# Batched matmul on one core: x loaded behind the weights of its group, and cast by row pairs ahead of the copies of that group

## The chip, the cores and the metric

The kernel runs on one core of one Trainium2 chip. Times are device microseconds of one launch. A run is "fast" or "slow" by its granted clock and span. Each comparison was made on one chip in alternating rounds. A ratio is the mean time of one kernel's fast runs over that of the kernel before in the same rounds, so it is not quite the ratio of the medians that are quoted.

## The reference

128 independent products of a 256 x 512 matrix by a 512 x 384 matrix, all float32:

```
b1, b2, m, k, n = 8, 16, 256, 512, 384
x: (b1, b2, m, k)   weight: (b1, b2, k, n)
out = np.matmul(x, weight).astype(np.float32)
```

x has 67.1 MB, the weights 100.7 MB, the output 50.3 MB: 218 MB that must pass between HBM and the core.

## The kernel before

Four products make a group (G = 4), so there are 32 groups. One group is one x tile (2.10 MB), two halves of weights (1.57 MB each) and one output tile (1.57 MB). All transfers are issued by SyncE, in one queue, in the order of the program; what is issued may run ahead of the computation as far as buffers allow (two x tiles, four weight halves, four output tiles).

```
def load(e, t, U, s):
    n = t * U + s
    if not isinstance(n, int) or n >= XS:
        e.wait_ge(x_cast, n + (1 - XS))
    e.dma_start(x_sb[s % XS][:], ...).then_inc(x_in[s % XS], 16)
    for d in range(G // D):                      # two halves of the weights
        ...
            e.wait_ge(w_cast, ...)
        e.dma_start(w_sb[slot][:], ...).then_inc(w_in[slot], 16)

def on_sync(e):
    ...
        for s in range(U):
            load(e, t, U, LAG + s)               # LAG = 4
            store(e, t, U, s)
```

So the queue holds x, weights, weights, store, again and again. ScalarE casts x of the next group between two output copies of the group at hand:

```
def cast_x(e, t, U, s):                          # two instructions of 2048 elements
    e.wait_ge(x_in[s % XS], ...)
    e.wait_ge(t_made, n * T + ((1 - BS) * T + BIAS))
    for h in range(S):
        ins = e.copy(out=x_bf[s % BS][:, :, h], in_=...)
    ins.then_inc(x_cast, 1)

def step(t, U, s, more):                         # ScalarE, one group
    for q in range(T):                           # T = 4 row pairs
        copy_out(e, t, U, s, q)
        if q == 1 and more:
            cast_x(e, t, U, s + 1)
```

TensorE transposes the cast x (16 instructions a group, by way of PSUM tile `pt`), VectorE copies the transposed x back (`x_t`) and casts the weights (`w_bf`), TensorE multiplies into PSUM tile `po` (128 matmuls a group), and ScalarE copies the result out (`out_sb`), from which it is stored.

## Time and profile before

| | before |
|---|---|
| time, median of 3 runs | 519.87 us (519.76 to 519.98) |
| span of the profiled run | 517.8 us |
| packets' share of 16 DMA engines' span | 99.3% |
| mean rate | 421 GB/s |
| TensorE, VectorE, ScalarE busy | 61%, 63%, 41% |

The columns are line, engine, operation, output and input, count; then the busy time in us and the mean ns of one; then the idle time ahead of them and what ended it:

```profile
L182 PE MATMUL po<-w_bf,x_t 128*32 128x384 bf16 x4096 | 231.4, 400 | 121.4 <-DVE x_t L155 121.4
...
L168 PE MATMUL pt<-identity,x_bf 128*128 128x128 f32 x512 | 82.8, 325 | 74.3 <-ACT x_bf L131 74.3
L131 ACT CAST x_bf<-x_sb 128x2048 bf16<-128x2048 f32 x64 | 118.5, 1901 | 7.3 <-DMA x_sb<-in_x_dram 7.3
...
L131 ACT ACT_TABLE_LOAD x1 | 1.3, 1283 | 1.3 <-PEq L232 1.3
```

TensorE waits for the transposed x before its matmuls (121.4 us over 32 groups), and ScalarE hardly ever waits for x (7.3 us, once, at the start), because x arrives ahead of its weights.

### The profile page before, as it was taken

What the parts mean: (1) busy time and instruction counts of PE and PEld (TensorE: products, weight loads), DVE (VectorE), ACT (ScalarE), POOL (GpSimd) and SP (SyncE); (2) the same over time, 40 slices, a digit from 0 to 9 for tenths busy, and PEclk for the clock granted to TensorE, in tenths of its full rate; (3) what the DMA queues carried; (4) which work ended last, traced back from release to release, by engine and by line L of the source; (5) the groups of instructions that cost most, each with busy time, mean ns of one, the idle gap of its engine ahead of it and who ended that gap; (6) DMA issues with size and microseconds to landing.
All of it is one profiled execution on the core that took longest, in us unless ns stands there. A gap on an engine that the chain in (4) does not pass through costs nothing.

```text
span 517.8 us, 11229 instructions
## 1 busy us (share of the span) xinstructions
PE 314.3 (61%) x4608; PEld 198.2 (38%) x4608; DVE 323.9 (63%) x384; ACT 212.9 (41%) x193; POOL 0.7 (0%) x6
## 2 busy tenths in 40 slices
PE   0588674576655676555766557665566655676653
PEld 0455443343433443333434334343344333443432
DVE  0788867655577555775556765557755577555670
ACT  3156462454324553245533345523455233553332
POOL 0000000000000000000000000000000000000000
PEclk9988896787868886787878678866877686777867
DMA  8999999999999999999999999999999999999995
GB/s 332 433 423 428 425 431 429 429 431 424 428 431 430 428 427 429 429 429 430 431 424 431 429 433 426 426 431 427 432 429 428 427 430 428 432 430 426 428 430 233
DMA packets 18869, 218.18 MB, mean 421 GB/s; under 512 B 2096, under 2 KB 2096, under 8 KB 2608
## 3 DMA queue, kind: packets, MB, share of 16 engines
q1 hardware_dynamic: 18864, 218.11, 99.3%
q8 instruction: 3, 0.05, 0.0%
q14 instruction: 2, 0.02, 0.0%
HBM read 167.77 MB, written 50.33 MB: 421 GB/s over the span
## 4 chain that ended last, share of the span: by engine, by line
DMA 81%; DVE 13%; issue 2%; PE 2%; ACT 1%; SPq 0%; DVEq 0%; ACTq 0%
DMA w_sb<-in_weight_dram 81%; DVE w_bf L149 12%; PE po L182 2%; ACT x_bf L131 0%; DVE x_t L155 0%; SPq L109 0%; ACT out_sb L196 0%; SPq L101 0%; DVEq L144 0%; DVEq L226 0%; SPq L108 0%; ACTq L195 0%; SPq L290 0%; SPq L55 0%
## 5 line engine op out<-in xcount | busy, mean ns | idle before, releaser
L149 DVE CAST w_bf<-w_sb 64x1536 bf16<-64x1536 f32 x256 | 244.5, 955 | 179.1 <-DMA w_sb<-in_weight_dram 172.1
L182 PE MATMUL po<-w_bf,x_t 128*32 128x384 bf16 x4096 | 231.4, 400 | 121.4 <-DVE x_t L155 121.4
L196 ACT COPY out_sb<-po 128x768 f32<-128x768 f32 x128 | 99.4, 803 | 289.3 <-PE po L182 289.3
L182 PEld LDWEIGHTS po<-w_bf,x_t 128*32 128x32 bf16 x4096 | 124.8, 116 | 225.3 <-DVE x_t L155 131.1
L168 PE MATMUL pt<-identity,x_bf 128*128 128x128 f32 x512 | 82.8, 325 | 74.3 <-ACT x_bf L131 74.3
L131 ACT CAST x_bf<-x_sb 128x2048 bf16<-128x2048 f32 x64 | 118.5, 1901 | 7.3 <-DMA x_sb<-in_x_dram 7.3
L168 PEld LDWEIGHTS pt<-identity,x_bf 128*128 128x128 f32 x512 | 73.3, 213 | 86.1 <-issue 86.1
L155 DVE COPY x_t<-pt 128x1024 bf16<-128x1024 bf16 x128 | 79.4, 683 | 1.0
L131 ACT ACT_TABLE_LOAD x1 | 1.3, 1283 | 1.3 <-PEq L232 1.3
masks.py:199 POOL TENSOR_SCALAR_AFFINE_SELECT identity<-identity 128x128 f32<-128x128 f32 x1 | 0.3, 294 | 0.2 <-POOL identity L202 0.2
L202 POOL MEMSET identity<- 128x128 f32 x1 | 0.2, 205 | 0.5 <-SPq L55 0.5
L279 POOL MEMSET const-bfloat16-1.0<- 128x1 bf16 x1 | 0.1, 102 | 0.0
L279 POOL MEMSET const-uint8-127<- 128x1 uint8 x1 | 0.1, 102 | 0.0
L279 POOL MEMSET const-float32-0.0<- 128x1 f32 x1 | 0.1, 99 | 0.2 <-issue 0.2
L279 POOL MEMSET const-float32-1.0<- 128x1 f32 x1 | 0.1, 99 | 0.0
## 6 DMA issues: line engine op xcount, KB each, us to landing
w_sb<-in_weight_dram SPq DMA_DIRECT2D x64, 1536.0 KB, 27.5
x_sb<-in_x_dram SPq DMA_DIRECT2D x32, 2048.0 KB, 25.8
out_dram<-out_sb SPq DMA_DIRECT2D x31, 1536.0 KB, 30.6
out_dram<-out_sb SPq DMA_DIRECT2D x4, 384.0 KB, 4.0
```

The source lines that it names most:

```text
L131: ins = e.copy(out=x_bf[s % BS][:, :, h], in_=x_sb[s % XS][:].rearrange("p r (q s c) -> p r s q c", s=S, c=KO)[:, :, h],)
L149: e.tensor_copy(out=w_bf[(s * G + d * D + a) % WBS][h * HP : (h + 1) * HP], in_=w_sb[slot][a * HP : (a + 1) * HP, h * KO : (h + 1) * KO, : ...
L155: e.tensor_copy(out=x_t[s % TS][:, 2 * q : 2 * q + 2], in_=pt[(s * T + q) % PT][:].bitcast(bf16),).then_inc(t_copied, 1)
L168: ins = e.transpose(pt[(s * T + q) % PT][:, rr, h, :], words[:, 2 * q + rr, h :: KO // 2], identity[:],)
L182: ins = e.matmul(po[(s * T + q) % PO][mine, rr, :N], x_t[s % TS][:, 2 * q + rr, ko // 2, mine, ko % 2], w_bf[(s * G + i) % WBS][:, ko, :], ...
L196: e.copy(out=out_sb[s % OS][:, 2 * q : 2 * q + 2, :], in_=po[(s * T + q) % PO][:, :, :N],).then_inc(o_copied, 1)
L202: e.memset(identity[:], 0.0).then_inc(id_done, 1)
L279: nc = _bacc.Bacc("TRN2", target_bir_lowering=False, num_devices=1)
```

## The change

The intent: a store is to be followed by weights and not by x, and x is to be cast where it is used, in four pieces of a row pair each, so that TensorE can start on the first piece. The diff, cut to its core:

```
     def load(e, t, U, s):
         n = t * U + s
-        if not isinstance(n, int) or n >= XS:
-            e.wait_ge(x_cast, n + (1 - XS))
-        e.dma_start(x_sb ...)
         for d in range(G // D):
             ...                                  # weights, unchanged
+        if not isinstance(n, int) or n >= XS:
+            e.wait_ge(x_cast, n * T + (1 - XS) * T)
+        e.dma_start(x_sb ...)

-    def cast_x(e, t, U, s):                      # whole group, two halves
+    def cast_x(e, t, U, s, q):                   # one row pair
+        if q == 0:
+            e.wait_ge(x_in[s % XS], ...)
+        e.wait_ge(t_made, n * T + (q + 1 - T + BIAS))
+        rows = slice(2 * q, 2 * q + 2)
+        e.copy(out=x_bf[s % BS][:, rows], in_=...).then_inc(x_cast, 1)

     def multiply(e, t, U, s):
-        e.wait_ge(x_cast, n + 1)
         for q in range(T):
+            e.wait_ge(x_cast, n * T + (q + 1))

     # ScalarE
-        cast_x(e, 0, NG, 0)
-        with e.Fori(0, NG // U - 1) as t: ...    # copies 0, 1, cast of the next group, copies 2, 3
+        with e.Fori(0, NG // U) as t:
+            for s in range(U):
+                for q in range(T):
+                    cast_x(e, t, U, s, q)
+                for q in range(T):
+                    copy_out(e, t, U, s, q)
```

## The prediction

> **What bounds the kernel now.** I read the page first, then the windows view by stage, then the waits of the compute engines and of the DMA queue, and last the timeline of one group in the middle. The page:
>
> ```profile
> span 517.8 us, 11229 instructions
> ...
> PE 314.3 (61%) x4608; PEld 198.2 (38%) x4608; DVE 323.9 (63%) x384; ACT 212.9 (41%) x193; POOL 0.7 (0%) x6
> ...
> DMA  8999999999999999999999999999999999999995
> ...
> DMA packets 18869, 218.18 MB, mean 421 GB/s; under 512 B 2096, under 2 KB 2096, under 8 KB 2608
> ...
> q1 hardware_dynamic: 18864, 218.11, 99.3%
> ...
> DMA 81%; DVE 13%; issue 2%; PE 2%; ACT 1%; SPq 0%; DVEq 0%; ACTq 0%
> ```
>
> The reader is to see three things. No compute engine is busy over 63%. The DMA row is 9 in 38 of 40 slices, and packets fill 99.3% of the 16 engines' span. The chain is 81% DMA. A chain can run through a transfer that only queues, so the share of DMA in it would not be enough alone; the windows view settles it:
>
> ```profile
> 4.00:30.00 26.00, 10.73 (x144) 7.15 (x144) 14.06 (x17) 7.78 (x6) 0.00 (x0) 1.00 1.01 429
> 30.00:60.00 30.00, 20.91 (x324) 15.08 (x328) 25.50 (x31) 15.72 (x15) 0.00 (x0) 0.88 1.00 425
> ...
> 100.00:490.00 390.00, 242.62 (x3508) 150.21 (x3512) 247.73 (x295) 159.22 (x145) 0.00 (x0) 0.77 1.01 429
> ...
> 505.00:517.80 12.80, 4.95 (x100) 2.60 (x92) 0.00 (x0) 3.23 (x4) 0.00 (x0) 0.77 0.56 231
> ```
>
> The last two columns are the DMA share and GB/s: 1.01 and 429 through the whole middle, so the engines never run out of packets there. One group moves 2.10 MB of x, 3.15 MB of weights and 1.57 MB of output, 6.82 MB in all; at 429 GB/s that is 15.9 us, and the timeline's period between two groups' stores is 16.1 us. In the trace's packet records a weight or store packet (12,288 bytes) takes 460 ns and an x packet (16,384 bytes) 611 ns almost without exception: all time above those minima adds up to 3.1 us per engine over the run, 1 us of it in the first 20 us. So no gap shows where a store is followed by x.
>
> The queue is also far ahead of the need:
>
> ```profile
> w_sb<-in_weight_dram SPq DMA_DIRECT2D x64, 1536.0 KB, 27.5
> x_sb<-in_x_dram SPq DMA_DIRECT2D x32, 2048.0 KB, 25.8
> out_dram<-out_sb SPq DMA_DIRECT2D x31, 1536.0 KB, 30.6
> ```
>
> A weight half moves in 3.7 us (1.57 MB at 429 GB/s), yet lands 27.5 us after its issue. Some 24 us, one and a half groups, stand in the queue before it. The issuing engine waits long (258.2 us for the x casts, 136.1 us for the weight casts in its waits), but while it waits the queue has work.
>
> **What the Trainium skill says.** "DMA: Bandwidth & Descriptors", section "Where 436 GB/s comes from", gives 435.2 GB/s as the ceiling of the ports between DMA engines and SBUF. "HBM Reference", section "Specifications (TRN2)", gives some 358 GB/s per core where both cores of a pair stream and about 425 for a core alone. The trace agrees with the second case: 429 GB/s with one core running, 1.4% under the ceiling. The DMA page's "Queues, rings and completion order" says that an engine consumes its descriptors in ring order; the landings agree, x, weights and store following one another at the pace of their bytes. "ScalarE: Activation LUTs", section "What ACT_TABLE_LOAD costs", gives 186 ns + 0.833 ns per element for an instruction with immediate operands, and some 93 ns of overlap back to back. For 2048 elements that is 1892 ns; the page of the profile has 1901 for the x cast, and two in a row take 3.70 us, so both agree.
>
> **The change, part by part.**
>
> 1. The order of loads: weights, x, store instead of x, weights, store. Bytes, packet sizes, the number of transfers and the single queue stay. Cost on the bounding resource: 0, unless a change of direction or size between packets costs something, and above it did not.
>
> 2. The x cast: two instructions of 2048 elements become four of 1024. By the skill's formula one takes 186 + 853 = 1039 ns (estimate); four in a row 4 x 1.04 - 3 x 0.09 = 3.9 us, against 3.70. That is 0.2 us per group, 6 us of ScalarE over 32 groups, on an engine 41% busy: not on the path.
>
> 3. Where the cast stands. Before, the cast of group n+1 stood after the second output copy of group n. Now the cast of n+1 follows all four copies of n. This makes a ring through ScalarE and TensorE: casts, transposes, matmuls, copies, next casts. The middle of the run gives the terms:
>
> ```profile
> 252.29 3.70 ACT L131 CAST x_bf<-x_sb 128x2048 bf16<-128x2048 f32 x2
> 253.95 7.86 DVE L149 CAST w_bf<-w_sb 64x1536 bf16<-64x1536 f32 x8 [5.50 <-DMA w_sb<-in_weight_dram]
> 255.89 1.50 ACT L196 COPY out_sb<-po 128x768 f32<-128x768 f32 x2
> ...
> 261.84 2.48 DVE L155 COPY x_t<-pt 128x1024 bf16<-128x1024 bf16 x4
> ...
> 262.58 8.02 PE L182 MATMUL po<-w_bf,x_t 128*32 128x384 bf16 x128 [4.28 <-DVE x_t L155]
> ```
>
> Ring: casts 3.9, the last row pair's transposes 0.6 (a quarter of 2.2), matmuls 8.0 (6.7 to 8.2 over the groups, as the granted clock varies), last copy 0.8, and some 0.1 for each of four hand-overs: 13.7 us. The transfers need 16.1. So the new serial ring fits, with 2.4 us to spare.
>
> 4. Does everything arrive in time? Call T the landing of a group's last load. Before, that is the second weight half: VectorE casts its four pieces until T + 4, copies the first transposed pair (0.7), and matmuls start at about T + 5. After, it is x: ScalarE casts until T + 4.0, the last transposes end at T + 4.7, and the transposed copies run beside the casts because VectorE is already through with the weights (halves land at T - 8.5 and T - 4.9, and eight casts take 7.9). Matmuls start at T + 4.8. The gain is 0.2 us and counts once, at the end of the run: the last load lands at 497.3 us, matmuls start at 502.3.
>
> 5. Buffers. Weight slots come free at about T - 4.6 and T - 0.7, x at T + 4.1, where before x came first. All are issued with well over 15 us of queue still before them (at T the queue still holds two stores and one whole group, 19.5 us, and then the new weights). At the head, I stepped through the first six groups: the least backlog I find is some 10 us. The before kernel has two slight dips near 36 and 43 us, 0.15 us together, which go.
>
> 6. The end: after the last load the stores of four older groups are queued (4 x 3.7 = 14.6 us, until about 512), so the tail too is mostly bytes; the last quarter of the last store follows the last copy.
>
> Sum: 0 in the middle, -0.15 at the head, -0.2 at the end, so 519.87 - 0.35 = **519.5 us**.
>
> **The rivals.**
>
> - *The serial ring becomes the bound.* For it: the cast and the copies now share one order with nothing between to fill TensorE, and the granted clock falls to 0.7 in places. Against it: 13.7 of 16.1 us. If I had forgotten 3.5 us per group, 1.1 us x 32 = 35 us would be lost, +7%. I think it unlikely, since every term was read from the trace.
>
> - *x frees its buffer late, the queue runs dry.* For it: the DMA queue's longest wait is already for the x cast, in-order issue makes weights and stores wait behind it, and x now needs its cast 4 us after landing. Against it: 24 us of queue. A dry queue of 0.5 us per group would make 16 us, +3%.
>
> - *The DMA engines run faster with a store followed by weights* (the intent). For it: packets of the same size follow each other there. Against it: packets already stand at their minimum; even at the ceiling of 435 GB/s the middle would gain 1.4%, 7 us. So this can hardly reach 2%.
>
> - *The transfer order is hidden altogether*: same time within 0.1%. That is close to my own sum, and likeliest.
>
> **Range and chances.** The three runs before lie within 0.22 us. Both small terms are under 0.5 us; packet service could move by some tenths of a per cent in either direction, and the tail by a us. I take 517.8 to 521.2. Faster by over 2% (below 509.5) is below what all bytes need at the present rate (218.2 MB at 429 GB/s is 508.6, plus 2 us before the first packet and 3 after the last): chance 0.01. Slower by over 2% needs one of the first two rivals: 0.03. Within 2%: 0.96.
>
> **What would show it.** DMA share 1.01 and 429 GB/s again between 100 and 490 us, packets at 460 and 611 ns (steps 1, 5). Casts x128 at about 1.04 us (step 2). ScalarE's wait for x a few us in every group, TensorE's transposes then following the casts, and matmuls some 4.8 us after x lands (steps 3, 4). VectorE waiting for transposes instead of only for weights. The prediction is wrong if the DMA row shows 7 or 8 in the middle (a dry queue or the ring), if ScalarE never waits for x (the ring is the bound), or if the packets' own times change.

## The result, and the profile after

| | before | after |
|---|---|---|
| time, median of 4 runs | 519.92 us (519.76 to 519.98) | 518.66 us (518.09 to 519.12) |
| ratio | | 0.9976 (95%: 0.9958 to 0.9993) |
| span of the profiled run | 517.8 us | 517.2 us |
| TensorE, VectorE, ScalarE busy | 61%, 63%, 41% | 59%, 64%, 46% |

A second measurement, in the rounds of the first experiments, gave 519.80 and 518.77 us, ratio 0.9980 (0.9966 to 0.9993). The change gains 0.20 to 0.24 per cent, 1.0 to 1.3 us. The predicted time was 519.5 us, a gain of 0.35.

The middle of the run in the windows view of the changed kernel (columns: window and its length, then busy us and count of TensorE's matmuls, its weight loads, VectorE, ScalarE and GpSimd, then the granted clock, the DMA share and GB/s):

```profile
100.00:490.00 390.00, 239.35 (x3556) 156.70 (x3558) 254.31 (x294) 181.25 (x203) 0.00 (x0) 0.78 1.01 429
```

The last two numbers are those of the kernel before: 1.01 and 429. The lines of the page that answer to those shown of before:

```profile
L166 PE MATMUL pt<-identity,x_bf 128*128 128x128 f32 x512 | 123.7, 425 | 199.3 <-ACT x_bf L132 199.1
L180 PE MATMUL po<-w_bf,x_t 128*32 128x384 bf16 x4096 | 185.1, 342 | 1.0 <-issue 1.0
...
L132 ACT CAST x_bf<-x_sb 128x1024 bf16<-128x1024 f32 x128 | 124.4, 1042 | 80.9 <-DMA x_sb<-in_x_dram 80.8
...
L132 ACT ACT_TABLE_LOAD x8 | 10.3, 1283 | 42.9 <-DMA x_sb<-in_x_dram 42.9
```

TensorE's wait has moved from the matmuls (121.4 us before, now 1.0) to the transposes (199.3 us), which now follow x directly. The matmuls became shorter (400 to 342 ns) and the transposes longer (325 to 425 ns). The Trainium skill explains it in "TensorE: Matmul & The Clock Gate", section "Part 1: The HAM clock gate (the "warmup" mystery)": after an idle window of some 3.4 us TensorE runs at half clock until it has been busy for about as long. The trace agrees: before, the idle 4 us stood in front of the matmuls, and in the group whose matmuls start at 278.65 us the trace's clock record is at 0.5 from 278.2 to 281.6 us, over the first 3 us of them; now the idle time stands in front of the transposes, and in the group shown next the record is at 0.5 from 272.5 to 279.3 us, over all the transposes and the first 0.9 us of the matmuls. None of this work is itself on the path that sets the time; when it runs will matter below.

One group in the middle of the changed kernel's timeline (start, length, what; in brackets the idle time ahead of it and its end):

```profile
273.31 3.89 ACT L132 CAST x_bf<-x_sb 128x1024 bf16<-128x1024 f32 x4 [2.41 <-DMA x_sb<-in_x_dram]
274.49 3.97 PE L166 MATMUL pt<-identity,x_bf 128*128 128x128 f32 x16 [4.44 <-ACT x_bf L132]
...
278.39 5.81 PE L180 MATMUL po<-w_bf,x_t 128*32 128x384 bf16 x128
```

The casts start when x lands, the first transposes follow 1.2 us later, and the matmuls begin 5.1 us after the landing.

**Where does the gain come from?** Not from the mean rate, which is the same. The end of the run shows it. Windows view of the kernel before, last columns granted clock, DMA share, GB/s:

```profile
505.00:511.00 6.00, 4.95 (x100) 2.60 (x92) 0.00 (x0) 3.23 (x4) 0.00 (x0) 0.84 0.91 377
511.00:513.00 2.00, 0.00 (x0) 0.00 (x0) 0.00 (x0) 0.00 (x0) 0.00 (x0) 1.00 0.77 306
513.00:516.00 3.00, 0.00 (x0) 0.00 (x0) 0.00 (x0) 0.00 (x0) 0.00 (x0) 0.62 0.07 30
```

and of the changed kernel:

```profile
505.00:511.00 6.00, 1.87 (x48) 1.01 (x40) 0.00 (x0) 1.72 (x3) 0.00 (x0) 1.00 0.99 410
511.00:513.00 2.00, 0.00 (x0) 0.00 (x0) 0.00 (x0) 0.00 (x0) 0.00 (x0) 0.60 0.48 191
```

A DMA share of 0.07 is one engine of sixteen (0.06) at work: in the last 3 us of the kernel before, essentially one engine still has packets and the others have none. **The time is set by the last of the 16 DMA engines, and one engine is late.** Each transfer adds 16 to its semaphore, one for each engine, and the trace records the landings. From them I take for every transfer the lag: the last of the 16 landings less their median. (The trace does not name the engine of a landing, so "the late engine" is whichever is last.) Groups and stores are counted from 0. For the last load of the last group:

```
                        median of 16 engines     last engine     lag
before (weights)              493.85 us           497.25 us      3.4 us
after  (x)                    493.76 us           496.55 us      2.8 us
last store: before 516.4 us, after 515.8 us
```

The median engine gains 0.1 us, the late engine 0.7, and that is what the profiled runs differ by (0.6). The lag of before is 1.5 us in the first group, stays there until about group 12, and then grows by 0.1 us a group; after, it stays at 1.7 to 1.8 us until about group 20. So the question for the experiments is what makes the late engine lose more time.

### The profile page after: what moved, and what is told of

It is laid out like the page before. It is cut to its first block, busy times and chain, and to the rows that moved or that the text cites. A ratio compares the mean times of both kernels' runs of the same rounds, so it can differ in the third digit from the quotient of the medians.

```text
span 517.2 us, 11523 instructions
## 1 busy us (share of the span) xinstructions
PE 306.6 (59%) x4608; PEld 200.6 (39%) x4608; DVE 332.8 (64%) x384; ACT 236.7 (46%) x264; POOL 0.7 (0%) x6
## 4 chain that ended last, share of the span: by engine, by line
DMA 81%; ACT 10%; PE 4%; issue 3%; ACTq 0%; SPq 0%
DMA x_sb<-in_x_dram 81%; ACT x_bf L132 9%; PE po L180 2%; PE pt L166 1%; ACTq L130 0%; ACT out_sb L194 0%; SPq L111 0%; SPq L103 0%; ACT L132 0%; ACTq L193 0%; SPq L282 0%; SPq L55 0%
## 5 line engine op out<-in xcount | busy, mean ns | idle before, releaser
L166 PE MATMUL pt<-identity,x_bf 128*128 128x128 f32 x512 | 123.7, 425 | 199.3 <-ACT x_bf L132 199.1
L180 PE MATMUL po<-w_bf,x_t 128*32 128x384 bf16 x4096 | 185.1, 342 | 1.0 <-issue 1.0
L166 PEld LDWEIGHTS pt<-identity,x_bf 128*128 128x128 f32 x512 | 91.8, 216 | 232.1 <-issue 218.3
L194 ACT COPY out_sb<-po 128x768 f32<-128x768 f32 x128 | 102.2, 798 | 147.2 <-PE po L180 147.2
L153 DVE COPY x_t<-pt 128x1024 bf16<-128x1024 bf16 x128 | 88.4, 691 | 122.3 <-PE pt L166 121.8
L132 ACT CAST x_bf<-x_sb 128x1024 bf16<-128x1024 f32 x128 | 124.4, 1042 | 80.9 <-DMA x_sb<-in_x_dram 80.8
L180 PEld LDWEIGHTS po<-w_bf,x_t 128*32 128x32 bf16 x4096 | 108.8, 101 | 73.8 <-issue 14.2
L132 ACT ACT_TABLE_LOAD x8 | 10.3, 1283 | 42.9 <-DMA x_sb<-in_x_dram 42.9
## 6 DMA issues: line engine op xcount, KB each, us to landing
w_sb<-in_weight_dram SPq DMA_DIRECT2D x64, 1536.0 KB, 27.5
x_sb<-in_x_dram SPq DMA_DIRECT2D x32, 2048.0 KB, 27.5
```

The lines of the kernel that those rows point to most:

```text
L132: e.copy(out=x_bf[s % BS][:, rows], in_=x_sb[s % XS][:, rows].rearrange("p r (q s c) -> p r s q c", s=S, c=KO),).then_inc(x_cast, 1)
L153: e.tensor_copy(out=x_t[s % TS][:, 2 * q : 2 * q + 2], in_=pt[(s * T + q) % PT][:].bitcast(bf16),).then_inc(t_copied, 1)
L166: ins = e.transpose(pt[(s * T + q) % PT][:, rr, h, :], words[:, 2 * q + rr, h :: KO // 2], identity[:],)
L180: ins = e.matmul(po[(s * T + q) % PO][mine, rr, :N], x_t[s % TS][:, 2 * q + rr, ko // 2, mine, ko % 2], w_bf[(s * G + i) % WBS][:, ko, :], ...
L194: e.copy(out=out_sb[s % OS][:, 2 * q : 2 * q + 2, :], in_=po[(s * T + q) % PO][:, :, :N],).then_inc(o_copied, 1)
```

## The experiments

Twelve kernels ran. Three theories stood at first: the order of packets (a store followed by weights costs the late engine less), the place of the casts, and the start (weights as the first transfers).

### One half of the change at a time

**order_only**: the kernel before with only the two blocks of `load` exchanged; the casts keep their place and their two instructions.

```
     def load(e, t, U, s):
         n = t * U + s
-        (x block)
         for d in range(G // D): ...
+        (x block)
```

> The kernel before with the new load order alone (weights, x, store); the cast stays where it was. Packet-order theory (the lagging DMA engine loses less per group where a store is followed by weights): most of the gain is here, ratio 0.9965 to 0.9985, about 518.7 us. Cast theory (the place of the casts gives the gain): ratio 0.9995 to 1.0005. Start theory (weights as the first transfers start faster): ratio about 0.998, with the gain already there when group 8's loads have landed.

Measured: 518.09 us (518.03 to 518.59, 5 runs) against 519.80, ratio 0.9971 (0.9957 to 0.9984).

**casts_only**: the changed kernel with x put back in front of the weights in `load`; the casts are by row pairs ahead of the copies.

> The changed kernel with the old load order (x, weights, store). Packet-order theory: ratio 0.9995 to 1.001, no gain. Cast theory: ratio 0.997 to 0.9985. Start theory: no gain.

Measured: 520.21 us, ratio 1.0009 (0.9995 to 1.0023).

**after_again**: the changed kernel in the same rounds.

> The changed kernel once more, on the same chip and in the same rounds as the three others. All theories: ratio 0.996 to 0.999, about 518.7 us. If it comes out within 0.9995 to 1.0005, the gain of the first measurement was chance.

Measured: 518.77 us (518.56 to 518.82), ratio 0.9980 (0.9966 to 0.9993). So the gain is no chance, it belongs to the order of the loads, and the new place of the casts adds nothing to it. The order alone is, if anything, better than the whole change: all its runs but one lie below all of the changed kernel's in the same rounds. The start theory expected the gain to be there when group 8 has landed; the median and last engines of the changed kernel stand at the same time as before there (127.9 and 129.7 against 127.9 and 129.5 us, by the last packets of that group's loads), so by this measure it falls. The measure sees only the engine that is last at that moment; what it misses is told under "The same measure in every kernel".

**store_before_x**: the changed kernel, but each store is issued between the weights and the x of a later group. The ring of transfers is then weights, weights, store, x: as a ring the same as before, though the x that follows the store now belongs to the group whose weights went ahead.

```
                 load(e, t, U, LAG + s)           # weights alone
                 store(e, t, U, s)
+                load_x(e, t, U, LAG + s)
```

> The changed kernel with the store issued between a group's weights and the next x, so that in the ring of transfers a store is followed by x again (weights, weights, store, x), as in the kernel before, though x still comes behind its own weights. Packet-order theory: no gain, ratio 0.9995 to 1.0005, and the slowest DMA engine loses some 0.03 us more per group than in the changed kernel. Cast theory and start theory: ratio about 0.998.

Measured: 530.21 us (530.01 to 530.61), ratio 1.0202 (1.0188 to 1.0216). **All three theories fell here**: one had expected no gain, two a gain, none 10 us of loss. The windows view shows the loss, and who has it:

```profile
100.00:490.00 390.00, 231.91 (x3456) 151.02 (x3456) 247.61 (x287) 177.21 (x198) 0.00 (x0) 0.77 1.01 428
504.00:508.00 4.00, 2.32 (x60) 1.23 (x48) 3.84 (x6) 2.17 (x3) 0.00 (x0) 1.00 0.14 59
...
511.50:520.00 8.50, 7.24 (x76) 4.75 (x80) 2.77 (x4) 4.68 (x5) 0.00 (x0) 0.57 0.06 25
```

In the middle all is as ever (1.01, 428 GB/s). At the end one engine works alone for 8.5 us (0.06). Its part of the last x landed only at 511.5 us, 14.2 us behind the median, and TensorE's last group had to wait for it. Its lag was 1.9 us in the first group and 14.2 us in the last. While it is alone the packet records can only be its own: its store packets of 12,288 bytes take 464 to 531 ns, where the median packet of this size takes 460.

### What slows the late engine: what follows the store, or where it stands against the computation?

**store_mid**: the kernel before, casts untouched, with the store between the two weight halves: x, weights, store, weights. A store is then followed by weights, though x comes first.

```
-                load(e, t, U, LAG + s)
-                store(e, t, U, s)
+                load(e, t, U, LAG + s, ("x", 0))
+                store(e, t, U, s)
+                load(e, t, U, LAG + s, (1,))
```

> The kernel before, casts where they were, with the store moved between the two halves of the weights: x, weights, store, weights. If what follows a store decides (x is bad, weights are good), ratio 0.996 to 0.9985 although x comes first. If it is x behind its weights that helps, ratio 0.9995 to 1.001. If the store's distance to the last load of a group decides (a store issued into the middle of a group is bad, as in store_before_x), slower, ratio 1.01 to 1.03.

Measured: 528.90 us, ratio 1.0177 (1.0163 to 1.0191); the lag grew from 1.5 to 12.4 us. So it is not what follows the store. In both orders tried, a store that stands ahead of the group's last load is bad, be that load x or weights. The computation is timed by the landing of the last load, so this says at which moment of the computation the late engine stores.

**transfers_store_x** and **transfers_store_w**: all casts, matmuls and copies taken out, stores of zeros, each load waiting only for the landing of the one before it in its buffer (results wrong). They differ in one line:

```
-        ORDER = [0, 1, 's', 'x']
+        ORDER = [0, 1, 'x', 's']
```

> The transfers alone, result wrong on purpose: no casts, no matmuls, the stores write zeros; each load waits only for the landing of the load before it in its buffer. Order weights, weights, store, x. If the late DMA engine is slowed by the other transfers alone, its lag grows here too (the last of 16 engines ends 5 us or more behind the median, run 8 to 15 us longer than its sister with store and x exchanged). If it is slowed by the compute engines' use of the buffers, the lag stays at 2 us and both orders take the same time within 0.1%. The bytes alone need 508.6 us at 429 GB/s.

> The transfers alone, result wrong on purpose, in the changed kernel's order: weights, weights, x, store. Under both theories the lag stays at about 2 to 3 us, and the run takes some 513 to 517 us; what tells them apart is the difference to the sister run.

Measured: 517.79 us (517.33 to 518.26) and 517.24 us (517.03 to 517.82), 0.1% apart, and in both the lag ends below 2 us. Without computation the two orders are worth the same; the 11.4 us that tell store_before_x from the changed kernel come with the computation. The pair also gives a floor: the changed kernel is 1.4 to 1.5 us over its transfers alone (taken on another chip, where the kernel before took 519.69 us).

### Which engine?

transfers_store_x once more, each time with one compute engine running the kernel's own kind of instruction on spare tiles, tied to no transfer (results wrong): TensorE the matmuls, VectorE the weight casts, ScalarE the output copies.

```
+    def busy(e):                                  # transfers_and_matmuls
+        with nc.Fori(0, 42, engines=...) as t:
+            for s in range(2):
+                for q in range(T):
+                    e.wait_ge(p_made, ...)        # its own earlier work
+                    (the 32 matmuls of a row pair, on tiles of zeros)
```

> transfers_store_x with TensorE alone running matmuls of the kernel's shape on tiles of zeros, tied to no transfer, through nearly the whole run; result wrong on purpose. transfers_store_x took 517.8 us with a lag of the last DMA engine of 1.9 us. If TensorE's reading of the buffers stretches the late engine's stores: lag of 5 us and more, 5 to 20 us longer. If it is another engine, or if none alone does it: 517 to 519 us, lag about 2 us.

> transfers_store_x with VectorE alone running the weight casts on a spare tile, tied to no transfer; result wrong on purpose. If VectorE's traffic stretches the late engine's stores: lag of 5 us and more, 5 to 20 us longer. If it is TensorE or ScalarE: 517 to 519 us.

> transfers_store_x with ScalarE alone running the output copies into spare tiles, tied to no transfer; result wrong on purpose. If ScalarE's traffic stretches the late engine's stores: lag of 5 us and more, 5 to 20 us longer. If it is TensorE or VectorE: 517 to 519 us.

Measured: with matmuls 528.34 us (528.10 to 528.86); with casts 517.57 us (517.33 to 517.67); with copies 517.94 us (median of 517.47, 517.84, 518.05 and one run of 521.08). **TensorE alone adds 10.5 us to the transfers, VectorE's casts and ScalarE's copies nothing that shows.** (The lags of the last two end at 2.3 and 2.7 us against 1.9, one trace each: some tenths of a us are not excluded.) Windows views of transfers_and_matmuls (columns here: TensorE's matmuls, its weight loads, GpSimd, clock, DMA share, GB/s):

```profile
50.00:460.00 410.00, 410.00 (x10100) 263.67 (x10096) 0.00 (x0) 1.00 1.01 428
...
511.00:514.00 3.00, 0.00 (x0) 0.00 (x0) 0.00 (x0) 0.50 0.23 98
514.00:525.00 11.00, 0.00 (x0) 0.00 (x0) 0.00 (x0) 0.50 0.06 26
```

and of transfers_store_x (GpSimd, clock, DMA share, GB/s):

```profile
50.00:460.00 410.00, 0.00 (x0) 1.00 1.01 428
...
511.00:514.00 3.00, 0.00 (x0) 1.00 0.44 188
514.00:516.00 2.00, 0.00 (x0) 1.00 0.03 12
```

Again one engine stands alone, for 11 us. Two details make the cause firm. The matmuls of this probe stop at 469.6 us, and the lag, which had grown by half a us a group from group 9 on, stops growing with them: 12.4, 13.0, 13.0, 13.0, 13.0 us for x of groups 27 to 31. And while the engine works alone after that, all its 23 store packets from 514 to 524.5 us take 460 ns: it is no slow engine, it is slow beside matmuls (464 to 531 ns in store_before_x). What of TensorE's work does it, reading tiles or writing PSUM, is not told apart. The fetching of its instructions is unlikely, as far as the trace records it: the instruction queues have four packets after the start.

### The same measure in every kernel

From the landings I took, for stores 8 to 27, how long the last engine needs for a store (its landing less the last landing of the transfer ahead), and from the trace how much of that time TensorE was busy. That share is taken 0.6 us earlier than the landings, since a landing is recorded some 0.5 us after the end of its packets (the last x of store_before_x: 511.00 and 511.48 us). It is rough: without the shift it is 0.25 for before and 0.57 for after.

```
kernel                   last engine's store   TensorE busy in it   its lag at store 8 / 27   median time
order_only                    3697 ns               0.00                2.2 / 2.2 us          518.09
transfers_store_x             3703 ns               0.00                1.6 / 1.9             517.79
two_more_casts                3721 ns               0.18                1.8 / 3.1             519.65
after_again                   3716 ns               0.41                1.7 / 2.6             518.77
after                         3728 ns               0.41                1.7 / 2.9             518.66
before                        3751 ns               0.41                1.7 / 3.4             519.80
casts_only                    3782 ns               0.65                2.0 / 4.3             520.21
transfers_and_matmuls         4081 ns               0.85                4.5 / 12.9            528.34
store_mid                     4076 ns               0.96                4.0 / 12.3            528.90
store_before_x                4155 ns               0.97                4.4 / 14.2            530.21
```

The more of its store lies beside TensorE's work, the longer it takes.

The last landing hides something, though: it need not be the same engine's all the time. Sort the 16 landings of each store and follow them from store to store (one trace of each kernel), and four stand apart. Before, at store 3, they are 1.25, 1.44, 1.50 and 1.53 us behind the median. At store 27 three of them are where they were (1.37, 1.44, 1.51), and the first has grown to 3.44, by 0.09 us a group; it passed the others at about store 7. After, the growing one goes from 0.72 to 2.85 us (0.50 to 2.58 in after_again), also by 0.09 us a group, and passes the others, at 1.7 to 2.0 us, at store 17 to 21. So the later onset of the lag after the change is a lower start and not a slower loss. From store 3 to 27 the growing engine loses, in ns a group: order_only 27 (it ends at 1.57 us and is never the last), two_more_casts 71, after_again 87, after 89, before 91, casts_only 128, and the three slow kernels at the foot 440 to 525 once it is last. Up to casts_only this rises with the share of TensorE in the table, and before and after agree in both. In transfers_and_matmuls the loss too starts before it shows: from 75 us on each group has a burst of 7 to 10 store packets of some 520 ns.

The three that stay behind are no matter of the stores: before, the trace has packets of 16 KB of the instruction queue at 6.2, 35.3 and 42.9 us, some 1.0 to 1.1 us each, and in the landings that follow each one more engine stands 1.5 us behind.

This gives the sizes. In order_only the growing engine ends at 1.57 us and not at 3.44, 1.5 us of it by the smaller loss ((91 - 27) ns x 24 groups). The last is then one of the three others, at 2.2, so some 1.2 us are left; the profiled spans differ by 1.5 and the medians by 1.7. For the changed kernel the loss a group is the same as before; of its gain of 1.0 to 1.3 us the lower start gives 0.5 to 0.75 (at store 3).

Why order_only is all but free of it can be read from its timeline. There the late engine's store follows its x directly and needs 3.7 us. ScalarE casts the whole x in that time, and TensorE idles:

```profile
257.92 3.70 ACT L131 CAST x_bf<-x_sb 128x2048 bf16<-128x2048 f32 x2 [4.01 <-DMA x_sb<-in_x_dram]
...
261.74 3.44 PE L168 MATMUL pt<-identity,x_bf 128*128 128x128 f32 x16 [6.09 <-ACT x_bf L131]
```

In the changed kernel the transposes begin 1.2 us after the first cast starts (the lines of group 273.31 above), so they run beside the second half of the store. By this reading (the pieces of the cast were not varied alone) the finer casts, which were to help, give back a part of what the order gains.

What stays open: that TensorE slows one engine's stores is shown, and that the order alone takes most of this loss away; but before and after lose the same, and no run says what sets the start that differs. Before, at 91 us, the growing engine falls back by 0.74 us at the moment of a packet of 8 KB of the instruction queue; two_more_casts, which loads in the order of the changed kernel, stands at 1.4 us at store 3, so the order alone doesn't set it. Whether weights as the first transfers matter is therefore not settled: when group 8's loads have landed, the growing engine of the changed kernel does stand 0.5 to 0.7 us better than before. Nor do the runs say why one engine alone is hit by TensorE, and its stores above all.

### The two rivals of the prediction

**two_more_casts** and **eight_more_casts**: the changed kernel with casts of the same size to spare tiles ahead of the real ones, in the ring of casts, transposes, matmuls and copies.

```
         rows = slice(2 * q, 2 * q + 2)
+        for v in range([1, 1, 0, 0][q]):          # eight: [2, 2, 2, 2]
+            e.copy(out=spare[...][:], in_=x_sb[s % XS][:, rows]...)
```

> The changed kernel with two casts more per group, to spare tiles, in the ring of casts, transposes, matmuls and copies: 2.0 us more in a ring that the changed kernel's trace shows to wait some 3.4 us per group for x. If the ring has that slack: same time, ratio to before 0.997 to 1.0, and the wait for x falls to about 1.5 us per group. If the serial ring were near the bound: up to 2.0 x 32 = 64 us longer, ratio up to 1.12.

Measured: 519.65 us, ratio 1.0002 (0.9986 to 1.0017), at the upper edge of what the slack was to give. ScalarE's waits for x:

```profile
ACT spare L134 <- DMA x_sb<-in_x_dram: 28.5, 16, 2.8
ACT L134 <- DMA x_sb<-in_x_dram: 27.9, 6, 17.7
```

Without the first wait of 17.7 us this is 38.7 us over 31 groups, 1.25 us each. In the changed kernel the two lines have 80.8 and 42.9 us, less 17.4 for the first, 3.4 us each. Two us of work went into the wait, as expected, and from group 8 on the mean period of a group is 15.88 us in both. The time is 0.9 us over after_again; in the trace the last output copy ends at 511.75 us against 507.72, so that the last store now waits for it. As far as the traces show, only the tail pays.

> The changed kernel with eight casts more per group in its ring. Per group the ring is 15.9 us of transfers less 3.4 us of wait for x, so 12.5 us; eight casts at 0.95 us back to back make it 20.1 us, against 15.9 us of transfers: about 32 x 4.2 = 134 us longer, some 650 us, ratio 1.25, ScalarE never waiting for x, and the DMA share of the middle at 0.8. If the ring theory is wrong and casts hide elsewhere: below 560 us.

Measured: 680.54 us, ratio 1.3086. After the first group ScalarE never waits for x, and the DMA share falls:

```profile
100.00:300.00 200.00, 106.11 (x1348) 62.78 (x1340) 98.59 (x115) 148.09 (x161) 0.00 (x0) 0.66 0.85 332
```

The period is 20.5 us, close to the 20.1 expected; the whole run is 162 us longer instead of 134, partly because the first groups, which ran at 10.8 to 14.6 us in the changed kernel while no stores were due, now need 20 as well. So the serial ring is a real bound, 3.4 us away.

## Why the prediction was right

The predicted range, 517.8 to 521.2 us, holds both medians, and the chance of "within 2%" was where the result fell. The bound, and with it "about the same time", was rightly reasoned; that the sum came within a us is luck. Neither of its two small terms came as told (steps 5 and 6), and what the change gained came from a term that was put at 0. Step by step:

- **What bounds the kernel: right.** DMA share 1.01 and 429 GB/s in the middle, before and after. The probes with transfers alone put the floor at 517.2 us.
- **Step 1, the order of loads, was put at "0, unless a change of direction or size between packets costs something". This is the term that was mis-sized**: it measured 1.7 us for the order alone and 1.0 to 1.3 us for the whole change. The proof was read from the mean over 16 engines. I had summed all packets' excess over their minimum, 3.1 us per engine, and saw no gap where a store is followed by x. The sum stands (though 15% of the 12,288-byte packets took over 465 ns, so that "460 ns almost without exception" is loose), and both hide that one engine had more than its share and that the end waits for that one. For the order alone the cause is also not in the transfers: it lies in what TensorE does while the late engine stores. For the whole change it is in part open.
- **Step 2, four casts of 1.04 us, 3.9 us in a row: right** (1042 ns, 3.89 us). What it missed: ScalarE's table load, once before, now comes eight times, 1283 ns each, once in each pass of the loop of four groups, whose first instruction is now a cast. The 1283 ns that the Trainium skill gives in "ScalarE: Activation LUTs", section "What ACT_TABLE_LOAD costs", hold. Each load starts 0.1 us after x has landed, so in those eight groups casts, transposes and matmuls come 1.3 us later; the queue is far enough ahead that no cost in time shows.
- **Step 3, the ring of 13.7 us with 2.4 us to spare: right in its verdict, too long by 1.2 us.** It measured 15.9 - 3.4 = 12.5. The matmuls take 5.8 us a group on average (185.1 / 32) and not 8.0, because TensorE now comes to most of them at full clock.
- **Step 4, matmuls 4.8 us after x lands: right** (5.1 us, and 6.4 in a group with a table load).
- **Step 5, buffers: right for the queue** (weights and x land 27.5 us after their issue). The two dips near 36 and 43 us, which were to go, are still there in the packet records, at 36 and 42 us; they are worth about 0.1 us. They are the packets of the instruction queue (36.3 and 42.6 us after the change), which an order of loads does not take away.
- **Step 6 and the 0.2 us at the end: wrong, without weight.** The last matmuls start 0.8 us earlier and the last copy ends 3.1 us earlier, yet the last store lands only 0.6 us earlier, as the queue still holds the stores ahead of it.
- **The rivals.** The serial ring and the dry queue did not come; eight_more_casts shows what the first would have looked like. "The DMA engines run faster with a store followed by weights" got its sign right and its reason wrong: store_mid has that very order and loses 9 us.

## What to carry to other kernels

Where a kernel is bound by transfers, look at the slowest DMA engine and not at the mean of the sixteen: the tail of the windows view, where the DMA share stands at one sixteenth, shows how many us one late engine costs. Look at the other late landings too: the last one can be another engine's, and hides a loss until it is overtaken. It is worth trying to place stores so that they are on the move while TensorE is idle; here this was worth 1.7 us in one direction and 10 us in the other, with the same bytes and the same queue. And an order of transfers that looks neutral in the queue may still shift the transfers against the computation, so measure it alone: half of this change (the order) measured 0.7 us faster than the whole in the same rounds.

## What the Trainium skill lacked or had wrong

- "SBUF — State Buffer", section "SBUF: two separate sides", says: "A DMA cannot be slowed by a compute op, and vice versa." The transfers alone took 517.8 us, and 528.3 us with nothing but matmuls beside them; one DMA engine's store packets took 464 to 531 ns beside matmuls and 460 without. The runs do not show whether SBUF is where they meet. Beside VectorE's casts (517.6 us) and ScalarE's copies (517.9 us) the sentence held.
- "DMA: Bandwidth & Descriptors" says in "Latency and other measured facts" that two of the engines are usually slower and ties it, as a best guess, to descriptors that GpSimd writes. Here SyncE issued every transfer, and four of the sixteen landings were still late by 1.3 to 1.6 us in group 8 (before), three of them each since a 16 KB packet of the instruction queue, and one by up to 14 us at the end (store_before_x). The trace does not number them.
- No page says that ScalarE's table load comes again in each pass of a loop that begins with such an instruction, after the wait for its input: x1 before, x8 in the changed kernel, 1283 ns each.
